# A two-layer hybrid decoder on one core: the 16x16 inverse in two halves of 8, and another order of the work beside it

## The chip, the core and the metric

The kernel runs on one core of a Trainium2 chip. Its time is device time in microseconds; the median of three runs is 1308.17 (1307.17 to 1308.69). The core has a matmul engine (PE; its weight loads are shown as PEld), a vector engine (DVE), a scalar engine (ACT), a general engine (POOL) and a queue that starts transfers (SP). Each works off its own list of instructions in order and waits on semaphores for the others.

## The reference, cut to what matters

256 tokens of width 1024 go through two layers, then a last norm. A layer is

```
x += 1/2 * SwiGLU(norm(x))
P  = norm(x) @ W_in                     # columns: RWKV-7 heads | MoBA q, k, v
x += concat[rwkv7(P_rwkv), moba(P_moba)] @ W_out
x += CrossAttn(norm(x), norm(mem))      # 4 heads over 256 memory tokens
x += 1/2 * SwiGLU(norm(x))
```

RWKV-7 has 8 heads of 64. For each head and token, with state S of 64x64:

```
S_t = S_{t-1} * decay_t + (S_{t-1} (-kk_t)) b_t^T + v_t k_t^T ;   y_t = S_t r_t
```

then a norm per head, a bonus term sum(r k r_k) v and a gate. MoBA has 8 heads of 64; with 256 tokens there is one block, so it is causal attention with a bias that depends on the distance of the tokens: softmax(q k^T / 8 + bias) v.

## The kernel before

**Matmuls.** Weights and activations are split into a high and a low part; a product is three matmuls (high x high, high x low, low x high). `load` fetches 1 MB of weights with one transfer on SP into one of two `raw` buffers, `unit` splits it in two halves of 1024 columns: ACT copies the high part (`whi`, line 83), DVE subtracts for the low part (`wlo`, line 77). `BANK(tag)` gives one of 8 PSUM banks: four `acc` for the dense products, two `tr` and two `pm`.

**RWKV in chunks.** The 256 tokens are four chunks of 64 (`rwkv`, line 568). `shifted` projects and mixes with the token before; `k, r, v, a, g` are tiles of 128 partitions (two heads of 64) by 4 pairs by 256 tokens. `kk` is normalized k; its squares `sq` are summed on PE into `pn`. `G` and `Gi` hold the decays and their inverses. `BK` (decayed keys) and `ZL` (decayed kk and r) are multiplied per chunk and head into 64x128 pair products, which masks (`C_MB`, `C_MK`) turn into `XB` and a part of `ZL` (lines 679 to 691).

A chunk needs the inverse of a triangular 64x64 matrix, 32 of them in all (4 chunks by 8 heads). `UD`/`UT` bring the 16x16 diagonal blocks into one layout, 128 partitions by 16 by 16 (`ub` the block, `mb` the inverse, from the identity), and all of them are inverted at once, one row after the other, lines 722 to 730:

```
for i in range(14, -1, -1):
    n = 15 - i                      # n == 1 is a copy
    tt(pr[:, 0:n, 0:n], mb[:, i + 1:16, i + 1:16], ub[:, i, None, i + 1:16] broadcast, mult)
    tensor_reduce(mb[:, i + 1:16, i:i + 1], pr, add)
    yield XI
```

`M` and `W2` are the inverses in matmul form; four steps of 32x32 matmuls (`p1`, `p2`/`p3`, `p4`, `p5`, line 762 on) combine them into 64x64 inverses `W`, first for chunks 0 and 1 (`cp = 0`), then for 2 and 3. Then `BV` (the bonus), and chunk by chunk: `from_state(0)` into `R`, `W` times `R`, `from_state(1)`, `BT` into the next state, `XB` for the output; after every second chunk the norm per head and the turn back into `yT`.

**The order of the work.** `rwkv` is a generator that yields, after each step, an amount of time that dense work may fill; `mix` (line 885) adds it up and takes pieces from a second generator until it is used up:

```
else:
    due += w
    while due > 0:
        due -= next(fill, 1e9)
```

Until the pair products are done the fill is `early`, MoBA's q and k projections. At `yield None` memory is split into an operand (`mem_operand`), and the fill becomes `others`: a piece of MoBA (`att`: `scores`, `turned`, `values` for each of four pairs of heads), after each a half unit of memory's keys (`late`, 24 matmuls of 256 columns), then memory's values `v_block(mT, 0)` (four pieces of 12 matmuls of 512 columns), then the first units of the output projection `og`. `v_block(mT, 1)` comes with the cross attention. A planner finally orders each engine's list by this order, and takes something later first where it reckons an engine would wait. `issue_after(i)` makes instructions queue behind `i` on its engine.

Of the kernel before, what the change touches and what calls it, by code (L numbers as in the profile page):

```python
# [16 lines left out]
S = 256  # L17
# [11 lines left out]
XI, XM, XC, XG = 0.3, 3.0, 1.2, 1.0  # L29
# [18 lines left out]
def body(tc, ctx, I, out):  # L48
# [27 lines left out]
    def tt(out_, a, b, op):  # L76
        V.tensor_tensor(out=out_, in0=a, in1=b, op=op)  # L77
# [7 lines left out]
    def split(hi, lo, src):  # L85
        c = copy(hi, src)
        tt(lo, src, hi.bitcast(FT), OP.subtract)
        return c.ins

# [305 lines left out]
    def mem_operand(m):  # L395
        mT = XT()
        for j in range(4):
            put_pair(mT, j, m[j // 2][:, 2 * (j % 2):2 * (j % 2) + 2, :])
        return mT
# [72 lines left out]
    def moba_bias():  # L472
        rel, oh = table
        u = SM([8, 384], name="u", tag="k2")
        V.memset(u[:, 256:384], NEG)
        p = BANK("pm")
        mm(p[0:8, 0:S], rel, oh)
        copy(u[:, 0:S], p[0:8, 0:S])
        nc.gpsimd.dma_start(scr_t, u)
        t = scr_t[:, :]  # L480
        nc.gpsimd.dma_start(scr_b, bass.AP(tensor=t.tensor, offset=t.offset, ap=[[0, 128], [1, 8 * 384]]))

    def moba(qT, kT, v, yT):
# [16 lines left out]
        def scores(p):  # L500
            load_bias(p + 1)
            s = [BANK("acc") for _ in range(2)]
            for t in range(2):
                for e in range(2):
                    r = half(e)
                    mm(s[e][:, cols[t]], qT[p // 2][r, p % 2, t * 128:(t + 1) * 128],
                       kT[p // 2][r, p % 2, 0:(t + 1) * 128])
            probs[p] = []
            for e in range(2):
                lg = SM([128, 384], name="lg", tag="k4")  # L510
                for t in range(2):
                    stt(lg[:, cols[t]], s[e][:, cols[t]], 0.125, bias[p][:, e, 128 * (1 - t):S],
                        OP.mult, OP.add)
                m = SM([128, 2], name="m", tag="n2")
                z = SM([128, 2], name="z", tag="n2")
                for t in range(2):
                    V.tensor_reduce(m[:, t:t + 1], lg[:, cols[t]], axis=AX.X, op=OP.max, negate=True)
                    A.activation(lg[:, cols[t]], lg[:, cols[t]], AF.Exp, bias=m[:, t:t + 1],  # L518
                                 accum_out=z[:, t:t + 1])
# [48 lines left out]
    def rwkv(l, xT, yT):  # L568
# [32 lines left out]
        for j in range(2):  # L601
            ac = BANK("acc").rearrange("p (c t) -> p c t", c=2)
            for c in range(2):
                p = 2 * j + c
                mm(ac[:, c, :], ups[:, 512 + p * 128:512 + (p + 1) * 128], wa[:, 1, :])
            for c in range(2):
                copy(G1[:, 2 * j + c, :], ac[:, c, :], scale=X(8, 2 * j + c))
            copy(g[:, 2 * j:2 * j + 2, :], ac)
        shifted(2, k[:, 2:4])

# [5 lines left out]
        V.memset(G[:, :, :, 0:1], 1.0)  # L616
# [44 lines left out]
        for cp in range(2):  # L661
            tt(BK[cp][:, :, :, 0:64], pv(a, cp), pv(Gi, cp), OP.mult)
            tt(BK[cp][:, :, :, 64:128], pv(km, cp), pv(Gi, cp), OP.mult)
        ZL = [[None, None] for _ in range(2)]
        for cp in range(2):
            Gp = G[:, :, 2 * cp:2 * cp + 2, :].rearrange("p c n t -> p n c t")
# [12 lines left out]
        for c in range(NCH):  # L679
            cp, cc = divmod(c, 2)  # L680
            pxs = [BANK(("pm", "tr")[cc]).rearrange("p (c t) -> p c t", c=4) for _ in range(2)]
            for p in range(4):
                for e in range(2):
                    hs = half(e)
                    mm(pxs[e][:, p, :], BK[cp][hs, cc, p, :], ZL[e][cp][hs, cc, p, :])
            for e in range(2):
                hs, ho = half(e), half(1 - e)
                px = pxs[e]
                tt(XB[cp][hs, cc], px[0:64], con[hs, None, C_MB:C_MB + 128].to_broadcast([64, 4, 128]),
                   OP.mult)  # L690
                tt(ZL[e][cp][ho, cc], px[64:128],
                   con[ho, None, C_MK:C_MK + 128].to_broadcast([64, 4, 128]), OP.mult)
# [14 lines left out]
        ub, mb, pr = (SM([128, 16, 16], name=n, tag="k1") for n in ("ub", "mb", "pr"))  # L707
# [4 lines left out]
        V.tensor_copy(mb, con[:, C_EYE:C_EYE + 256].rearrange("p (a b) -> p a b", a=16))  # L712
# [9 lines left out]
        for i in range(14, -1, -1):  # L722
            n = 15 - i
            if n == 1:
                V.tensor_copy(mb[:, 15, 14:15], ub[:, 14, 15:16])
                continue
            tt(pr[:, 0:n, 0:n], mb[:, i + 1:16, i + 1:16],
               ub[:, i, None, i + 1:16].to_broadcast([128, n, n]), OP.mult)
            V.tensor_reduce(mb[:, i + 1:16, i:i + 1], pr[:, 0:n, 0:n], axis=AX.X, op=OP.add)
            yield XI  # L730
        M, W2 = (SM([128, 16, 32], name=n, tag="k2") for n in ("M", "W2"))
        for z, zz in ((mb.rearrange("p a b -> p b a"), M), (mb, W2)):
# [3 lines left out]
            V.transpose(zz.rearrange("p n (b i) -> p i n b", b=2), ex.rearrange("p i b j -> p (i b j)"))  # L736
        W = H([128, 16, 64], name="W")
        for e in range(2):
            V.memset(W[e * 64 + 32:e * 64 + 64, :, 0:32], 0.0)
# [17 lines left out]
        values(0)  # L757
        for e in range(2):
            V.memset(SV[0][half(e), :, e, 0, :], 0.0)
        hq = [slice(e * 64, e * 64 + 32) for e in range(2)]  # L760
        hr = [slice(e * 64 + 32, e * 64 + 64) for e in range(2)]
        for cp in range(2):
# [3 lines left out]
            p1 = BANK("pm")[:, 0:256].rearrange("p (c t) -> p c t", c=8)  # L766
# [5 lines left out]
            p3 = BANK("tr")[:, 0:256].rearrange("p (c t) -> p c t", c=8)  # L772
            p2 = BANK("pm")[:, 0:256].rearrange("p (c t) -> p c t", c=8)
# [20 lines left out]
            p5 = BANK("pm")[:, 0:256].rearrange("p (c t) -> p c t", c=8)  # L794
# [6 lines left out]

        for j in range(2):
# [7 lines left out]
        for c in range(NCH):  # L810
# [14 lines left out]
            values(c + 1)  # L825
# [27 lines left out]
            if cc == 0:  # L853
                y = SM([128, 2, 4, 64], name="y", tag="k2")
            copy(y[half(1), cc], pz[half(1), :, 0, :])
            copy(y[half(0), cc], pz[half(0), :, 1, :])
            if cc == 0:
                continue
# [25 lines left out]

    def mix(l, xT, post):
# [277 lines left out]
```

## Time and profile before

| | |
|---|---|
| median of three runs | 1308.17 us |
| profiled execution, its own time | 1309.38 us |
| its span, first to last instruction | 1307.4 us |
| PE busy | 1282.3 us (98%), 8710 matmuls |
| PEld busy | 1099.3 us (84%) |
| DVE busy | 919.9 us (70%), 1709 instructions |
| ACT busy | 761.1 us (58%), 1447 instructions |
| POOL busy | 58.0 us (4%) |
| mean granted clock of PE | 0.993 |

A busy matmul engine isn't one at its peak: matmuls overlap, and their ends are modelled. Where a helper records an operation, all its uses have one line (77 is `tt`, 80 `stt`, 83 `copy`, 94 `mm`), so a row is told by its tiles. The mixing stage with RWKV and MoBA lies at 204 to 408 us in the first layer and at 850 to 1050 in the second. In all that follows, times are us from the start of the span.

### The profile page before, as it was taken

How to read it: one execution, taken by the hardware profiler on the slowest of the kernel's cores; microseconds unless marked ns; L12 is line 12 of the kernel's file. 1: busy time of each engine (PE TensorE's matmuls, PEld its weight loads, DVE VectorE, ACT ScalarE, POOL GpSimd, SP SyncE). 2: the span in 40 equal slices, each digit the busy share in tenths (PEclk: the TensorE clock that was granted, in tenths of full speed). 3: DMA queues.
4: the chain of work that ended last, by engine and by line, in shares of the span. 5: the costliest groups of instructions: out<-in, count | busy, mean ns of one | idle time of the engine just before them, and what ended most of it. 6: DMA issues, size and time to landing. Idle time of an engine off the chain costs nothing.

```text
span 1307.4 us, 21984 instructions
## 1 busy us (share of the span) xinstructions
PE 1282.3 (98%) x8710; PEld 1099.3 (84%) x8710; DVE 919.9 (70%) x1709; ACT 761.1 (58%) x1447; POOL 58.0 (4%) x61
## 2 busy tenths in 40 slices
PE   8999999998999999999999999999999999999997
PEld 6888888997778888888888888899887798888886
DVE  6797557797688767765576665668976877766644
ACT  6656437658646565564465554474785555655543
POOL 0081000020000000000000000000200000000000
PEclk9999999998999999999999999999999999999999
DMA  7867663333235345555635556443442345355552
GB/s 276 322 233 252 210 225 130 130 129 123 107 129 179 129 144 195 191 194 188 230 129 193 192 178 222 165 135 124 138 155 82 130 161 177 131 192 194 181 176 94
DMA packets 34422, 224.36 MB, mean 172 GB/s; under 512 B 4328, under 2 KB 4752, under 8 KB 9104
## 3 DMA queue, kind: packets, MB, share of 16 engines
q1 hardware_dynamic: 31344, 212.93, 46.4%
q0 software_dynamic: 2400, 9.45, 2.1%
q8 instruction: 68, 1.11, 0.3%
q10 hardware_dynamic: 576, 0.59, 0.1%
q14 instruction: 34, 0.28, 0.1%
HBM read 219.80 MB, written 4.73 MB: 172 GB/s over the span
## 4 chain that ended last, share of the span: by engine, by line
PE 77%; DVE 11%; ACT 7%; DMA 2%; issue 2%; SPq 0%; ACTq 0%
PE acc L94 71%; PE pm L94 4%; DVE wlo L77 3%; DMA raw<-in_w_f1i_dram 2%; DVE ZL L77 2%; ACT whi L83 1%; PE tr L199 1%; DVE XB L77 1%; DMA raw<-in_w_k_dram 1%; ACT BT L83 1%; ACT lg L518 1%; DVE wb L77 0%; ACT W L83 0%; DVE rkv L80 0%; DVE z L77 0%
## 5 line engine op out<-in xcount | busy, mean ns | idle before, releaser
L94 PE MATMUL acc<-xt,whi 128*128 128x512 f32 (+1 forms) x2496 | 685.0, 345 | 3.1 <-DVE lg L80 2.4
L77 DVE TENSOR_TENSOR wlo<-raw,whi 128x1024 fp32r<-128x1024 f32 (+1 forms) x456 | 465.3, 1036 | 260.5 <-ACT whi L83 259.0
L83 ACT ACTIVATE whi<-raw 128x1024 fp32r<-128x1024 f32 (+1 forms) x456 | 403.7, 905 | 325.5 <-PE acc L94 234.7
L94 PE MATMUL acc<-xt,wlo 128*128 128x256 f32 x1888 | 532.2, 283 | 2.2 <-DVE wlo L77 2.2
L94 PEld LDWEIGHTS acc<-xt,whi 128*128 128x128 f32 x2496 | 435.2, 191 | 67.6 <-DVE lg L80 2.9
L94 PEld LDWEIGHTS acc<-xt,wlo 128*128 128x128 f32 x1888 | 360.2, 191 | 4.5 <-DVE wlo L77 3.7
L94 PE MATMUL acc<-whi,hT 128*128 128x512 f32 x704 | 220.6, 393 | 0.0
L94 PEld LDWEIGHTS acc<-whi,hT 128*128 128x128 f32 x704 | 132.3, 188 | 30.0
L94 PE MATMUL acc<-wlo,hT 128*128 128x512 f32 x352 | 138.3, 393 | 0.0
L94 PEld LDWEIGHTS acc<-wlo,hT 128*128 128x128 f32 x352 | 66.2, 188 | 14.7
L77 DVE TENSOR_TENSOR z<-acc,z 128x256 f32<-128x256 f32 x160 | 66.8, 417 | 2.2 <-ACT z L83 2.2
L94 PE MATMUL acc<-wb,xt 128*128 128x512 f32 x240 | 62.0, 400 | 0.0
L83 ACT ACTIVATE z<-acc 128x256 f32<-128x256 f32 x160 | 58.5, 366 | 2.9 <-PE acc L94 2.9
L94 PE MATMUL acc<-whi,xt 128*128 128x512 f32 x160 | 53.4, 408 | 2.5 <-ACT whi L83 2.0
L83 ACT ACTIVATE xt<-tr,par 128x128 fp32r<-128x128 f32 x112 | 38.5, 365 | 27.9 <-PE tr L199 16.2
L94 PEld LDWEIGHTS acc<-wb,xt 128*128 128x128 f32 x240 | 43.3, 188 | 9.6 <-ACT xt L83 0.7
L174 ACT ACTIVATE junk<-x 128x512 f32<-128x512 f32 x36 | 22.7, 631 | 46.6 <-DVE x L80 25.2
L83 ACT ACTIVATE hT<-z 128x256 fp32r<-128x256 f32 x80 | 32.4, 405 | 18.6 <-DVE z L77 18.6
L77 DVE TENSOR_TENSOR z<-z,z 128x256 f32<-128x256 f32 x80 | 36.5, 456 | 7.3
L80 DVE SCALAR_TENSOR_TENSOR xt<-tr,par,xt 128x128 fp32r<-128x128 f32 x112 | 36.1, 345 | 7.8 <-ACT xt L83 7.8
L94 PE MATMUL acc<-whi,oT 128*128 128x512 f32 x128 | 40.3, 393 | 0.0
L94 PEld LDWEIGHTS acc<-whi,xt 128*128 128x128 f32 x160 | 29.9, 190 | 11.3 <-ACT whi L83 3.4
(249 smaller groups left out, 1224.0 us busy)
## 6 DMA issues: line engine op xcount, KB each, us to landing
raw<-in_w_f2i_dram SPq DMA_DIRECT2D x44, 1024.0 KB, 4.8
raw<-in_w_f1i_dram SPq DMA_DIRECT2D x42, 1024.0 KB, 4.9
raw<-in_w_f1o_dram SPq DMA_DIRECT2D x22, 1024.0 KB, 4.8
raw<-in_w_mixa_dram SPq DMA_DIRECT2D x22, 1024.0 KB, 4.8
raw<-in_w_f2o_dram SPq DMA_DIRECT2D x22, 1024.0 KB, 4.8
raw<-in_w_k_dram SPq DMA_DIRECT2D x8, 1024.0 KB, 4.8
raw<-in_w_v_dram SPq DMA_DIRECT2D x8, 1024.0 KB, 4.9
raw<-in_w_mixo_dram SPq DMA_DIRECT2D x8, 1024.0 KB, 4.9
```

The costliest lines, as they stand in the source:

```text
L77: V.tensor_tensor(out=out_, in0=a, in1=b, op=op)
L80: V.scalar_tensor_tensor(out_, a, s, b, op0=op0, op1=op1)
L83: return A.activation(out_, in_, AF.Copy, **k)
L94: nc.tensor.matmul(o, a, b, start=start, stop=stop, skip_group_check=True)
L174: marks["square"] = A.activation(junk, xt[:, n * 512:(n + 1) * 512], AF.Square, scale=1.0 / 32.0, accum_out=ss[:, n:n + 1]).ins
L199: nc.tensor.transpose(p[:, k, :], xs[:, k * 128:(k + 1) * 128], ident)
L518: A.activation(lg[:, cols[t]], lg[:, cols[t]], AF.Exp, bias=m[:, t:t + 1], accum_out=z[:, t:t + 1])
```

## The change

- The inverse treats each 16x16 block as two 8x8 blocks on the diagonal, inverted both at a time (views `ud`, `md`, sizes 2 x n x n, n up to 7), and the 8x8 block below as a product of three, two passes of 512 elements each with a reduction. `ub` and `mb` lie in one tile.
- `others` now starts with `v_block(mT, 0)` and two units of keys; then MoBA, with a half unit of keys after every third piece. `XI` and `XM` change; the inverse yields `2 * XI` a step. The first product of the inverse queues behind `mem_operand`'s last subtraction.
- The second half of the 32x32 stage becomes a generator of its own, `second`, advanced one step after each yield of chunks 0 and 1. Its banks are `tr` instead of `pm`.
- The pair products: each 64x128 matmul becomes two of 64x64, so that all masked products of `XB` land in one bank and need one masking pass.
- `kk` and `sq` come ahead of the scan; `ZL` by full products and copies; `BV` in `km`'s buffer and behind the inverse; some memsets and copies go to POOL, `G1` to DVE.
- MoBA: the bias table is stored times 8, and one `tensor_tensor_reduce` adds it and finds the maximum; the division goes from ACT to DVE. `v_block(mT, 1)` sums in `pm`.

The diff, cut to its core:

```
-XI, XM, XC, XG = 0.3, 3.0, 1.2, 1.0
+XI, XM, XC, XG = 0.8, 2.6, 1.2, 1.0
...
+            marks["memory"] = tt(mT[j][:, :, 1, :], src, mT[j][:, :, 0, :].bitcast(FT), OP.subtract).ins
...
-                for t in range(2):
-                    stt(lg[:, cols[t]], s[e][:, cols[t]], 0.125, bias[p][:, e, 128 * (1 - t):S],
-                        OP.mult, OP.add)
...
-                    V.tensor_reduce(m[:, t:t + 1], lg[:, cols[t]], axis=AX.X, op=OP.max, negate=True)
+                    V.tensor_tensor_reduce(lg[:, cols[t]], s[e][:, cols[t]], bias[p][:, e, 128 * (1 - t):S],
+                                           -0.125, -NEG, OP.add, OP.min, m[:, t:t + 1])
...
-                    copy(lg[:, cols[t]], lg[:, cols[t]], scale=z[:, t:t + 1])
+                    V.tensor_scalar(lg[:, cols[t]], lg[:, cols[t]], z[:, t:t + 1], None, op0=OP.mult)
...
+            tt(two(kk), two(kk), Gp(0), OP.mult)
+            tt(two(rG), two(r), Gp(1), OP.mult)
...
-                tt(ZL[e][cp][hs, :, :, uc(e)], pv(kk, cp)[hs], Gp[hs, :, :, 0:64], OP.mult)
-                tt(ZL[e][cp][hs, :, :, dc(e)], pv(r, cp)[hs], Gp[hs, :, :, 1:65], OP.mult)
+                copy(ZL[e][cp][hs, :, :, uc(e)], pv(kk, cp)[hs])
+                copy(ZL[e][cp][hs, :, :, dc(e)], pv(rG, cp)[hs])
...
-                    mm(pxs[e][:, p, :], BK[cp][hs, cc, p, :], ZL[e][cp][hs, cc, p, :])
+                    for i in range(2):
+                        mm(pxs[i][half(e ^ i), p, :], BK[cp][hs, cc, p, half(i)], ZL[e][cp][hs, cc, p, :])
+            tt(XB[cp][:, cc], pxs[0], con[:, None, C_MB:C_MB + 128].to_broadcast([128, 4, 128]), OP.mult)
...
-        for i in range(14, -1, -1):
-            n = 15 - i
+        for i in range(6, -1, -1):
+            n = 7 - i
...
+            pr = SM([128, 2, n, n], name="pr", tag="k1")
+            with after([marks["memory"]] if n == 2 else []):
+                tt(pr, md[:, :, i + 1:8, i + 1:8],
+                   ud[:, :, i, None, i + 1:8].to_broadcast([128, 2, n, n]), OP.mult)
+            V.tensor_reduce(md[:, :, i + 1:8, i], pr, axis=AX.X, op=OP.add)
+            yield 2 * XI
...
+        tt(pr, mb[:, hi, None, hi].to_broadcast([128, 8, 8, 8]),
+           ub[:, None, lo, hi].to_broadcast([128, 8, 8, 8]), OP.mult)
+        V.tensor_reduce(um2, pr, axis=AX.X, op=OP.add)
+        yield 2 * XI
...
+        V.tensor_reduce(mb[:, hi, lo], pr, axis=AX.X, op=OP.add)
...
-        for cp in range(2):
+        def inverse(cp):
...
-            p1 = BANK("pm")[:, 0:256].rearrange("p (c t) -> p c t", c=8)
+            p1 = BANK("tr")[:, 0:256].rearrange("p (c t) -> p c t", c=8)
...
+        yield from inverse(0)
+        second = inverse(1)
+
+        BV = km
+        for p in range(4):
+            with after([marks["inverse"]]):
+                stt(BV[:, p, :], r[:, p, :], P(P_RK, p), km[:, p, :], OP.mult, OP.mult)
...
+        for c in range(NCH):
+            for w in chunk(c):
+                yield w
+                if c < 2:
+                    next(second, None)
...
-            acc = [BANK("acc") for _ in range(2)]
+            acc = [BANK(("acc", "pm")[n]) for _ in range(2)]
...
         def others(mT):
+            yield from v_block(mT, 0)
             ks = late(mT)
-            for w in att:
+            yield from islice(ks, 4)
+            for i, w in enumerate(att):
                 yield w
-                yield from islice(ks, 1)
+                if i % 3 == 1:
+                    yield from islice(ks, 1)
             yield from ks
-            yield from v_block(mT, 0)
```

## Rows read from the trace of the kernel before

**Rows 1.** The page's chain of work that ended last, by engine.
```profile
PE 77%; DVE 11%; ACT 7%; DMA 2%; issue 2%; SPq 0%; ACTq 0%
```
**Rows 2.** Whom PE waited for, whole span: total us, times, longest us.
```profile
PE acc L94 <- ACT mpT L83: 2.7, 2, 1.4
...
PE acc L94 <- DVE lg L80: 2.4, 2, 1.2
...
PE pm L94 <- ACT sq L625: 1.6, 2, 1.0
...
PE acc L530 <- DVE lg L80: 0.6, 2, 0.4
```
**Rows 3.** Stretches: length, busy PE, PEld, DVE, ACT, POOL (instructions), clock, DMA, GB/s.
```profile
240.00:250.00 10.00, 10.00 (x74) 10.00 (x74) 7.37 (x20) 6.38 (x12) 0.00 (x0) 0.83 0.39 141
255.00:290.00 35.00, 34.22 (x302) 32.88 (x301) 33.51 (x56) 17.69 (x25) 7.90 (x8) 1.00 0.36 122
...
300.00:310.00 10.00, 6.85 (x90) 5.85 (x89) 9.68 (x30) 9.91 (x25) 0.73 (x1) 1.00 0.40 132
310.00:320.00 10.00, 9.75 (x245) 8.15 (x232) 8.02 (x17) 7.62 (x20) 0.71 (x1) 0.84 0.62 216
320.00:330.00 10.00, 10.00 (x221) 9.37 (x220) 4.60 (x6) 6.80 (x14) 0.00 (x0) 0.82 0.19 63
...
340.00:377.00 37.00, 36.88 (x419) 27.34 (x415) 26.89 (x57) 21.20 (x42) 0.55 (x1) 1.00 0.22 73
...
901.00:936.00 35.00, 34.22 (x302) 32.87 (x301) 33.87 (x57) 17.81 (x25) 7.76 (x8) 1.00 0.38 127
...
946.00:956.00 10.00, 7.21 (x118) 6.38 (x119) 9.67 (x27) 9.91 (x24) 0.73 (x1) 1.00 0.40 131
```
**Rows 4.** Timeline of DVE: the first and the last step of the inverse.
```profile
288.57 0.16 DVE L77 TENSOR_TENSOR pr<-mb,ub 128x4 f32<-128x4 f32 x1
...
306.80 0.39 DVE L77 TENSOR_TENSOR pr<-mb,ub 128x225 f32<-128x225 f32 x1
```
**Rows 5.** Timeline around `sq`, ACT's and PE's: start, us, instruction, idle before.
```profile
232.00 1.04 ACT L619 ACTIVATE Gi<-Lc 128x1024 f32<-128x1024 f32 x1
...
237.43 1.06 ACT L625 ACTIVATE sq<-kk 128x1024 f32<-128x1024 f32 x1 [0.55 <-DVE kk L623]
...
238.54 1.95 PE L94 MATMUL pm<-con,sq 128*128 128x2 f32 x16 [0.96 <-ACT sq L625]
```
**Rows 6.** DVE's groups, 204 to 420: count, busy us, mean ns, idle before.
```profile
L77 DVE TENSOR_TENSOR ZL<-kk,G 64x512 f32<-64x512 f32 x4 | 2.7, 684 | 0.1
L77 DVE TENSOR_TENSOR XB<-pm,con 64x512 f32<-64x512 f32 x4 | 2.7, 684 | 0.1
```
**Rows 7.** Groups of DVE and ACT, 204 to 420: logits and the value copies.
```profile
L80 DVE SCALAR_TENSOR_TENSOR lg<-acc,bp 128x256 f32<-128x256 f32 x8 | 3.3, 414 | 0.0
L517 DVE TENSOR_REDUCE m<-lg 128x1 f32<-128x256 f32 x8 | 3.3, 407 | 0.0
...
L83 ACT ACTIVATE SV<-tr 64x512 f32<-64x512 f32 x8 | 4.7, 590 | 0.1
...
L83 ACT ACTIVATE lg<-lg,z 128x256 f32<-128x256 f32 x8 | 4.0, 497 | 0.0
```
**Rows 8.** Timeline of POOL: products of 256 columns.
```profile
75.47 8.59 POOL L386 TENSOR_SCALAR memG<-memT,par 128x256 f32<-128x256 f32 x5
```
**Rows 9.** Timeline of PE: pair products, and the steps of a chunk (two rows a matmul).
```profile
267.36 1.16 PE L94 MATMUL tr<-ZL,BK 64*128 64x128 f32 x16
268.45 0.50 PE L94 MATMUL acc<-xt,whi 128*128 128x256 f32 x2
...
360.81 0.68 PE L94 MATMUL pm<-R,W 64*64 64x64 f32 x16
361.42 0.69 PE L94 MATMUL pm<-SV,ZL 128*64 128x64 f32 x16
362.04 0.50 PE L94 MATMUL acc<-whi,xt 128*128 128x512 f32 x1
```

More of the change, by code (lines that the diff above doesn't have):

```diff
@@ L76, in tt @@
     def tt(out_, a, b, op):
-        V.tensor_tensor(out=out_, in0=a, in1=b, op=op)
+        return V.tensor_tensor(out=out_, in0=a, in1=b, op=op)
     def stt(out_, a, s, b, op0, op1):
@@ L88, in split, with in_two @@
         return c.ins
+    def in_two(z):
+        return z[:, 0:256], z[:, 256:512]
     def after(ins):
@@ L397, in mem_operand @@
         for j in range(4):
-            put_pair(mT, j, m[j // 2][:, 2 * (j % 2):2 * (j % 2) + 2, :])
+            src = m[j // 2][:, 2 * (j % 2):2 * (j % 2) + 2, :]
+            copy(mT[j][:, :, 0, :], src)
+            marks["memory"] = tt(mT[j][:, :, 1, :], src, mT[j][:, :, 0, :].bitcast(FT), OP.subtract).ins
         return mT
@@ L477, in moba_bias @@
         mm(p[0:8, 0:S], rel, oh)
-        copy(u[:, 0:S], p[0:8, 0:S])
+        copy(u[:, 0:S], p[0:8, 0:S], scale=8.0)
         nc.gpsimd.dma_start(scr_t, u)
@@ L606, in rwkv @@
             for c in range(2):
-                copy(G1[:, 2 * j + c, :], ac[:, c, :], scale=X(8, 2 * j + c))
+                V.tensor_scalar(G1[:, 2 * j + c, :], ac[:, c, :], X(8, 2 * j + c), None, op0=OP.mult)
             copy(g[:, 2 * j:2 * j + 2, :], ac)
         shifted(2, k[:, 2:4])
+        kk = H([128, 4, S], name="kk")
+        sq = H([128, 4, S], name="sq")
+        for p in range(4):
+            V.tensor_scalar(kk[:, p, :], k[:, p, :], X(0, p), None, op0=OP.mult)
+        A.activation(sq, kk, AF.Square, scale=1.0 / RS)
         Lc = H([128, 4, S], name="Lc")
@@ L663, in rwkv @@
             tt(BK[cp][:, :, :, 64:128], pv(km, cp), pv(Gi, cp), OP.mult)
+        rG = H([128, 4, S], name="rG")
         ZL = [[None, None] for _ in range(2)]
         for cp in range(2):
[L666 removed]
+            Gp = lambda i: G[:, :, 2 * cp:2 * cp + 2, i:i + 64]
+            two = lambda z: ch(z)[:, :, 2 * cp:2 * cp + 2, :]
+            tt(two(kk), two(kk), Gp(0), OP.mult)
+            tt(two(rG), two(r), Gp(1), OP.mult)
             for e in range(2):
@@ L706, in rwkv @@
         V.transpose(UT.rearrange("p i b j -> p (i b j)"), UD.rearrange("p i n c b -> p (i n c b)"))
-        ub, mb, pr = (SM([128, 16, 16], name=n, tag="k1") for n in ("ub", "mb", "pr"))
+        both = SM([128, 512], name="both", tag="k2")
+        ub, mb = (z.rearrange("p (a b) -> p a b", a=16) for z in in_two(both))
+        ud, md = (z.rearrange("p (x r) -> p x r", x=2)[:, :, c:c + 128].rearrange(
+            "p x (a b) -> p x a b", a=8)[:, :, :, c:c + 8] for z, c in ((both[:, 0:272], 0), (both[:, 240:512], 8)))
         par2 = [con[:, C_PAR + i:C_PAR + i + 1] for i in range(2)]
@@ L735, in rwkv @@
                 V.tensor_scalar(ex[:, :, b, :], z, par2[b], None, op0=OP.mult)
-            V.transpose(zz.rearrange("p n (b i) -> p i n b", b=2), ex.rearrange("p i b j -> p (i b j)"))
+            marks["inverse"] = V.transpose(zz.rearrange("p n (b i) -> p i n b", b=2), ex.rearrange("p i b j -> p (i b j)")).ins
         W = H([128, 16, 64], name="W")
         for e in range(2):
-            V.memset(W[e * 64 + 32:e * 64 + 64, :, 0:32], 0.0)
+            nc.gpsimd.memset(W[e * 64 + 32:e * 64 + 64, :, 0:32], 0.0)
         SV = []
@@ L757, in rwkv @@
         values(0)
+        values(1)
         for e in range(2):
-            V.memset(SV[0][half(e), :, e, 0, :], 0.0)
+            nc.gpsimd.memset(SV[0][half(e), :, e, 0, :], 0.0)
         hq = [slice(e * 64, e * 64 + 32) for e in range(2)]
         hr = [slice(e * 64 + 32, e * 64 + 64) for e in range(2)]
-        for cp in range(2):
+        def inverse(cp):
             ix = slice(cp * 8, cp * 8 + 8)
@@ L771, in rwkv @@
             yield XM
-            p3 = BANK("tr")[:, 0:256].rearrange("p (c t) -> p c t", c=8)
-            p2 = BANK("pm")[:, 0:256].rearrange("p (c t) -> p c t", c=8)
+            p2, p3 = (z.rearrange("p (c t) -> p c t", c=8) for z in in_two(BANK("tr")))
             for i in range(8):
@@ L800, in rwkv @@
             yield XM
+        yield from inverse(0)
+        second = inverse(1)
+        BV = km
+        for p in range(4):
+            with after([marks["inverse"]]):
+                stt(BV[:, p, :], r[:, p, :], P(P_RK, p), km[:, p, :], OP.mult, OP.mult)
         for j in range(2):
@@ L808, in rwkv, with chunk @@
             stt(BV[:, p, :], BV[:, p, :], P(P_LNB, p), g[:, p, :], OP.add, OP.mult)
-        for c in range(NCH):
+        ys = []
+        def chunk(c):
             cp, cc = divmod(c, 2)
@@ L824, in rwkv @@
             V.tensor_copy(R[half(1)], pz[half(1), :, 1, :])
-            values(c + 1)
+            if c:
+                values(c + 1)
             yield XC
@@ L857, in rwkv @@
             if cc == 0:
-                continue
+                return
             y = y.rearrange("p n c t -> p (n c) t")
```

38 lines of the change are left out of this document (15 added, 23 removed).

## The prediction

> **What bounds the kernel now.** I read the page's chain of waits first, then PE's own waits, then busy time by stretch, and went into single instructions only where these pointed. The chain lies 77% on PE [rows 1], so a microsecond saved elsewhere counts only where PE waits for it. PE's waits for MoBA are three entries, two occurrences each, one per layer: 2.7 us for `mpT` (turned probabilities), 2.4 and 0.6 us for `lg` (logits) [rows 2]. Together 5.7 us. Next, 1.6 us for `sq`. The stretches show why [rows 3]. From 255 to 290 (pair products beside dense fill) PE is busy 34.22 of 35 us although DVE is at 33.51: DVE is full, but PE has other work. From 300 to 310 (inverse on DVE, MoBA as fill) PE falls to 6.85 of 10 with DVE at 9.68 and ACT at 9.91: the fill itself needs the two engines that the inverse occupies. Layer 1 repeats it, 7.21 of 10 from 946. In 340 to 377 (recurrences beside dense products) PE is at 36.88 of 37. So what can be won are some 5.7 us of MoBA's waits, a few small ones, and stretches at half clock: the granted clock is 0.83 in 240 to 250, and 0.84 and 0.82 in 310 to 320 and 320 to 330, each next to narrow matmuls or waits.
>
> The profile's own execution took 1309.38 us (span 1307.4), 1.2 above the median 1308.17. The sum is made against 1309.4 and brought down by 1.2 at the end.
>
> **The inverse.** Now 14 steps of a product and a reduction, from 0.16 us each at 4 elements to 0.39 us at 225 [rows 4]: about 1.04 ns an element above a floor of 0.16. Summed over the sizes, 28 instructions take some 6.9 us. After: six steps with 8, 18, 32, 50, 72, 98 elements, 12 instructions of 0.16 to 0.26, some 2.4 us; and four of 512 elements, by the same slope 0.16 + 0.53 = 0.69, some 2.8 us. 5.2 against 6.9: 1.7 us of DVE and 12 instructions fewer, bounds 0 to 2.7. That alone moves the end by nothing, since PE is what ends late; the gain is from what runs beside it.
>
> **The fill.** Under the inverse PE gets four pieces of the value product and four of keys ahead of MoBA, instead of logits. These need only weight splits, as the fill of 255 to 290 does, where PE ran at 34.22 of 35. So all 5.7 us of waiting leave this place. They don't all leave the kernel: the same logits, exponentials, turns and products now stand between the steps of the state recurrences, with only four key pieces as dense work between them, and each step there ends on a DVE or ACT copy too. Bounds: all 5.7 stays away, or all returns. I take half, -2.9, as there is a key piece between every scores and its turn, but none between a turn and its values. By the Trainium skill (page "Trainium Kernel Development and Optimization", section "Performance Expectations") a matmul's busy time tells little and the busy share of weight loads is what to judge by. By that share, 32.88 of 35 as full rate and 5.85 and 6.38 of 10 in the two bad stretches, the loss is 6.6 us rather than 5.7 and half of it 3.3; the trace agrees in place and nearly in size.
>
> **Waits that are added.** The first product of the inverse must queue on DVE behind memory's four low halves (512 columns, so about 0.69 each, 2.8 us), and these wait for buffers that the last dense matmuls of the stretch before free. Behind it on DVE stands the rest of the inverse; PE waits for that only at its products, after six to eight dense pieces. So 0; if DVE's list outlasts the pieces, up to 2.8 us a layer. `BV` must queue behind the inverse's last transpose, and `W` gets its buffer only when `BV` has read r: W is first wanted two product steps later, 0. The weight loads on SP keep their number and size, values before keys; POOL's bias loads move with MoBA and nothing on POOL that is wanted in this stage queues behind them: 0.
>
> **Earlier key norms.** `kk` and `sq` are asked for ahead of the scan and exponentials. Now PE waits 0.96 us for a `sq` that ACT starts at 237.43; the copies of k's second half, from which it is made, queue on ACT behind the exponentials, the last at 232.00 [rows 5]. Without those in front the chain ends one exponential (1.04 us) or more earlier, which covers the wait. I take the whole 1.6 us of both layers [rows 2]: -1.6, bounds 0 and -1.6.
>
> **DVE ahead of the inverse.** The masks are applied once over 128 partitions instead of twice over 64: 4 x 0.68 us less a layer. Decayed `ZL` is made by 4 full products for 8 half ones (0.68 each [rows 6]), also 2.7 us less, and 8 copies on ACT of about 0.59 each [rows 7], 4.7 us, more. Four `BV` products move behind the inverse, memsets go to POOL, four `G1` scalings come from ACT to DVE (some 1.4 us). DVE's 33.51 of 35 [rows 3] falls to about 27, ACT's 17.69 rises to about 22: neither is then full. PE's idle 0.78 us in this stretch, twice (255 to 290 and 901 to 936), goes: -1.6, bounds 0 and -1.6. POOL's new work hides in its idle time; if not, the identity comes late by one pass, some 1.7 us for 256 columns (8.59 for five [rows 8]).
>
> **MoBA's softmax.** 16 additions and 16 maxima (0.41 us each for 256 columns, less for 128 [rows 7]) become 16 fused passes. The trace has no such pass: at least one, 0.41, at most both, 0.82. I take 0.5, as an addition is the nearer row. 16 scalings go from ACT (0.50) to DVE. DVE thus keeps its load and ACT is eased by some 7 us. PE: nothing beyond what the fill's term holds.
>
> **Pair products.** 8 matmuls of 64 rows by 128 columns a chunk become 16 of 64 by 64, for the same columns streamed: the array must hold four tiles at once to break even. A chunk now takes 1.09 us to the next matmul (267.36 to 268.45 [rows 9]). `R,W`, eight 64x64 matmuls on two tiles with 64 columns, takes 0.61 (360.81 to 361.42); twice the matmuls at twice the columns is at worst 4 x 0.61 = 2.44. So 0 to +1.35 a chunk, eight chunks: 0 to +10.8 us; nothing below zero, since four tiles at best stream as long as two did. `SV,ZL` takes 0.62 with two column tiles over the same rows, so tiles do run side by side in both directions; nearer the low end: +0.25 x 8 = +2.0.
>
> **Clock.** The half-speed stretch of 310 to 330 costs (0.16 + 0.18) x 10 = 3.4 us in the profiled execution, and follows the worst waits. With dense fill it may go: half, -1.7, bounds 0 and -3.4. That of 240 to 250 sits behind matmuls of two columns that stay: 0, bound -0.17 x 10 = -1.7 a layer if layer 1 has it too.
>
> **The tail.** MoBA's last pair now ends after the recurrences and the output projection waits for it. Cover: the last key piece and the second value product, which now uses other banks. 0; uncovered, turn, copy and product of one pair, about 2 us a layer.
>
> **Sum:** -2.9 - 1.6 - 1.6 + 2.0 - 1.7 = -5.8; 1309.4 - 5.8 = 1303.6, less 1.2: **1302 us**.
>
> **Rivals.**
> 1. *The waits move to the recurrences and grow.* Behind the first inverse lie 11 recurrence steps and 4 of the second inverse, each ended by a copy on an engine that now also runs all of MoBA. For it: 300 to 310 shows what MoBA beside a DVE chain does to PE. Against it: the chain there was 28 instructions long on one engine, and a recurrence step has one or two. At 0.5 us a step, 15 steps, two layers: +15, and none of the fill's or the clock's gain: 1309.4 + 15 - 3.2 + 2.0 - 1.2 = 1322. It decides from 0.2 us a step: 6 us, the whole gain.
> 2. *The pair products run two tiles at a time.* +10.8 in place of +2.0: 1311, slower. For it: `R,W` has two row tiles only, and no row shows four 64x64 tiles. Against it: `R,W` and `SV,ZL` together. The Trainium skill ("TensorEngine Tiling (Array Packing)", section "Gotcha 1: PSUM Pressure") says that different row tiles cannot access the same PSUM bank at once, and after the change they do, where before each had its bank. By that rule the price is this rival's. The trace speaks against it: `R,W` writes one bank from both row tiles, and is as fast as `SV,ZL`, which has no second row tile.
> 3. *All waits and the half-speed stretches go:* -5.7 - 3.2 - 3.4 - 3.4, products at no cost: 1309.4 - 15.7 - 1.2 = 1292.5.
> 4. *No net:* fill's waits return in full, the clock stays: -3.2 + 2.0: 1307.
>
> **Chances.** About 0.2% (2.6 us) can be told from no change. Forecast (1296 to 1305.5) 0.50; rival 3, 0.14; rival 4, 0.15; rival 2, 0.09; rival 1, 0.12, of which smaller sizes end at 1310 to 1316. Faster is the forecast and rival 3: 0.64; same rival 4 and the edge of 2: 0.17; slower the rest: 0.19. The range, 1291 to 1312, leaves out the far part of rival 1 and the extremes.
>
> **What would show it.** Right: no wait for `lg` or `mpT` under the inverse, PE above 9.4 of 10 there; no wait for `sq`; pair products near 1.1 to 1.4 us a chunk. Wrong: pair products at 2 us or more; DVE above 9 of 10 and PE below 9 in the recurrences; new half-clock stretches there; PE idle at the output projection.

## The result, and the profile after

The changed kernel took 1316.2 us (median; 1310.4 to 1318.2) beside 1308.69 for the kernel before on the same chip: ratio 1.0056, 95% interval 1.0029 to 1.0083. In a later session (e14 below) it was 1.0042, 1.0020 to 1.0063. So it is about half a per cent slower, where the forecast said faster. The profiled execution took 1312.45 us (span 1310.1, before 1307.4). Its mean granted clock is 0.993, and the four of the seven executions that took over 1316 us have 0.986 to 0.992, so the trace shows 2.7 us of a loss that is 7.5 in the median.

The chain by engine hardly moved [rows 1], but TensorE's waits did. The rows after, as in [rows 2] (total us, times, longest us):
```profile
PE tr L97 <- ACT T L83: 7.7, 4, 4.5
...
PE tr L97 <- DVE M L756: 3.1, 2, 1.6
PE tr L97 <- issue: 2.7, 1, 2.7
PE pm L97 <- ACT R L83: 2.4, 2, 1.4
PE acc L97 <- DVE xt L77: 1.6, 1, 1.6
...
PE pm L97 <- DVE z L523: 0.6, 2, 0.3
```
The waits for `mpT`, `lg` and `sq` are gone, 7.3 us; in their place stand `T` (the inverse's first copied product), `M` (what VectorE's inverse delivers; 1.0 before) and others, 18.1 us.

Next the stretches, first before and then after, from the first transposes of `BK` (the inverse's start) to the first product with `yr` (the output projection), layer 0 and layer 1; columns as in [rows 3]:
```profile
289.80:382.40 92.60, 88.92 (x1187) 73.03 (x1186) 68.74 (x161) 66.43 (x153) 3.99 (x6) 0.96 0.36 126
935.30:1025.40 90.10, 86.14 (x1187) 70.44 (x1186) 68.50 (x160) 66.15 (x153) 1.45 (x2) 1.00 0.33 112
```
```profile
285.20:381.60 96.40, 89.12 (x1194) 76.01 (x1193) 71.80 (x185) 59.32 (x135) 5.63 (x10) 0.96 0.35 121
928.60:1030.40 101.80, 89.64 (x1194) 76.12 (x1194) 73.57 (x186) 61.55 (x138) 3.10 (x6) 0.97 0.29 100
```
This one stage went from 182.7 to 198.2 us, 15.5 longer: TensorE's idle time in it rose from 7.6 to 19.4 us, its busy time from 175.1 to 178.8. What lies around it gave 12.8 back, nearly all in three places: the inverse starts 4.7 us earlier in layer 0 and is reached 3.5 us faster from there to layer 1, and the output projection behind is 2.3 and 2.0 us shorter, as less fill is left for it (198 and 197 products against 204 and 205). 15.5 - 12.8 is the 2.7 us between the spans. The loss is therefore in the stage of inverse and recurrences. 11.7 of the 15.5 us are layer 1's. There TensorE waits 4.45 us for `T`, and it stands 2.71 us where the profile shows nothing that it waits for:
```profile
956.37 0.84 PE L97 MATMUL tr<-T,W 32*32 32x32 f32 x29 [4.45 <-ACT T L83]
...
983.22 0.18 PE L97 MATMUL tr<-M,XB 32*32 32x32 f32 x1 [2.71 <-issue]
```

How the waits come about is read from three engines of layer 0. VectorE: the inverse starts (292.18) only behind memory's last split `xt`, and that behind a weight split that stood 2.19 us; `BV`'s four products by r (written into `km`) end at 306.77.
```profile
290.44 1.23 DVE L77 TENSOR_TENSOR wlo<-raw,whi 128x1024 fp32r<-128x1024 f32 x1 [2.19 <-ACT whi L83]
291.58 0.69 DVE L77 TENSOR_TENSOR xt<-memT,xt 128x512 fp32r<-128x512 f32 x1
292.18 0.16 DVE L77 TENSOR_TENSOR pr<-both 128x8 f32<-128x8 f32 x1
...
301.79 1.04 DVE L756 STREAM_TRANSPOSE M<-ex 128x512 f32<-128x512 f32 x1
...
305.19 1.58 DVE L80 SCALAR_TENSOR_TENSOR km<-rkv,par,km 128x256 f32<-128x256 f32 x4
```
ScalarE: weights that came late, and then the first split of memory's values, which starts 0.03 us after the last of `BV`'s four has ended. Nothing in that split needs `BV`'s result: `v` is being written into the buffer that r had. `T` is queued behind it.
```profile
289.35 1.06 ACT L83 ACTIVATE whi<-raw 128x1024 fp32r<-128x1024 f32 x1 [3.57 <-DMA raw<-in_w_k_dram]
...
306.80 0.60 ACT L83 ACTIVATE v<-acc 128x512 fp32r<-128x512 f32 x1 [2.56 <-DVE km L80]
307.30 1.05 ACT L83 ACTIVATE whi<-raw 128x1024 fp32r<-128x1024 f32 x1
308.37 2.40 ACT L83 ACTIVATE SV<-tr 64x512 f32<-64x512 f32 x4
310.79 0.38 ACT L83 ACTIVATE T<-tr 128x256 f32<-128x256 f32 x1
```
TensorE waits for `M`, then for `T`, and comes to chunk 0's product `R,W` at 339.32, where W is the last to arrive; that first product of the recurrences stood at 341.1 before.
```profile
302.97 0.74 PE L97 MATMUL tr<-M,UA 32*32 32x32 f32 x64 [1.65 <-DVE M L756]
...
311.23 0.83 PE L97 MATMUL tr<-T,W 32*32 32x32 f32 x29 [2.95 <-ACT T L83]
...
320.53 0.69 PE L97 MATMUL tr<-W,TB 32*32 32x32 f32 x32
...
339.32 0.29 PE L97 MATMUL pm<-R,W 64*64 64x64 f32 x2 [0.41 <-ACT W L83]
```
W is late because GpSimd clears its tile at 337.12 (layer 1: 985.94), although the products that fill it were done at 321:
```profile
337.12 1.09 POOL L759 MEMSET W<- 32x512 f32 x2 [5.99 <-issue]
```

**Theory H (slots).** Tag `e`, the scratch pool, has 14 buffers of 4 KB. Counted in the code, 14 tiles are alive at the inverse after the change: v, g, G1, G, km, r, four `ZL`, two `XB`, two `BT`. r and km are among them because `BV` moved behind the inverse. Three more are asked for: the two tiles of memory's values, which the new fill asks for first, and W. The slots come free as r (read by `BV`, 306.8), g (about 327) and v (about 336), and are given in the order of asking: first value tile, second value tile, W. **Theory F**, the rival, is the prediction's first: the recurrences have too little dense fill, whatever the slots.

### The profile page after: what moved, and what is told of

Its sections match the earlier page's. It is cut to its first block, busy times and chain, and to the rows that moved or that the text cites. A ratio compares the mean times of both kernels' runs of the same rounds, so it can differ in the third digit from the quotient of the medians.

```text
span 1310.1 us, 22248 instructions
## 1 busy us (share of the span) xinstructions
PE 1276.6 (97%) x8838; PEld 1101.1 (84%) x8838; DVE 910.0 (69%) x1697; ACT 756.7 (58%) x1423; POOL 51.3 (4%) x73
## 4 chain that ended last, share of the span: by engine, by line
PE 77%; DVE 10%; ACT 6%; DMA 3%; issue 3%; SPq 0%; ACTq 0%; DVEq 0%
PE acc L97 69%; PE pm L97 5%; DVE wlo L77 3%; ACT whi L83 2%; DMA raw<-in_w_f1i_dram 2%; PE tr L202 1%; PE tr L97 1%; DMA raw<-in_w_k_dram 1%; DMA raw<-in_w_mixa_dram 1%; ACT ZL L83 1%; ACT BT L83 1%; ACT UD L83 1%; ACT SV L83 0%; DMA raw<-in_w_o_dram 0%; ACT lg L521 0%
## 5 line engine op out<-in xcount | busy, mean ns | idle before, releaser
L83 ACT ACTIVATE xt<-tr,par 128x128 fp32r<-128x128 f32 x112 | 38.5, 366 | 28.5 <-PE tr L202 15.5
L77 DVE TENSOR_TENSOR hT<-z,hT 128x256 fp32r<-128x256 f32 x80 | 35.5, 443 | 3.2 <-ACT hT L83 3.2
L358 ACT ACTIVATE z<-z 128x256 f32<-128x256 f32 x80 | 32.7, 409 | 4.3 <-DVE z L77 4.3
```

Of the source, the lines that this page charges most:

```text
L77: return V.tensor_tensor(out=out_, in0=a, in1=b, op=op)
L83: return A.activation(out_, in_, AF.Copy, **k)
L358: A.activation(sums[0], sums[0], AF.Silu)
```

## The experiments

Medians in us, ratio to the kernel before on the same chip with its 95% interval; from the profiled run TensorE's waits for `T` in both layers, when W is cleared in layer 0, and the length of the stage above, both layers.

| kernel | median | ratio | T | W | stage |
|---|---|---|---|---|---|
| changed | 1316.2 | 1.0056 (1.0029 to 1.0083) | 7.7 | 337.1 | 198.2 |
| e14 changed again | 1311.6 | 1.0042 (1.0020 to 1.0063) | 9.2 | 336.7 | 196.2 |
| e9 no order | 1306.4 | 1.0010 (0.9991 to 1.0029) | 0.3 | 333.6 | 193.5 |
| e5 less room, 14 slots | 1305.9 | 0.9998 (0.9975 to 1.0021) | 4.7 | 334.7 | 189.4 |
| e10 BV early, 14 slots | 1303.4 | 0.9987 (0.9971 to 1.0003) | 0.3 | 334.3 | 188.4 |
| e13 15 slots | 1296.3 | 0.9927 (0.9905 to 0.9948) | 3.6 | 325.0 | 179.3 |
| e2 keys first, 14 slots | 1295.8 | 0.9936 (0.9914 to 0.9958) | none | 308.1 | 186.4 |
| e1 16 slots | 1293.7 | 0.9907 (0.9879 to 0.9935) | 1.3 | 307.3 | 178.0 |
| e11 keys first, 16 slots | 1289.4 | 0.9874 (0.9851 to 0.9897) | 0.4 | 288.8 | 171.6 |

The trace of e2 is of an execution of 1302.3 us, 6.5 above its median, so its stage is not to be set against that median.

**e1, sixteen slots.** Against the changed kernel:
```diff
-WB = 5
-HEAP = {"e": 14, ...
-SMALL = {"k1": 6, ...
+WB = 4
+HEAP = {"e": 16, ...
+SMALL = {"k1": 5, ...
```


> The changed kernel, whole, but the scratch pool of 4 KB buffers (tag e) has 16 slots in place of 14; the room comes from one weight buffer (5 to 4) and one small buffer (k1, 6 to 5). Theory H (slots): 14 tiles of that pool are alive at the inverse, because r and km now live until BV, which stands behind the inverse's last transpose; memory's two value tiles and W find no slot, the first split of the values holds ScalarE 2.56 us ahead of T, and W's clearing waits until v(rkv) is read at 336.7. With 16 slots TensorE's wait for T (3.1 and 4.6 us) falls under 1 us in both layers, GpSimd clears W before 312 (layer 0) instead of at 337.1, chunk 0's product with W starts 8 to 15 us earlier than 339.3, and the time is 1300 to 1308. Theory F (the fill is too thin in the recurrences, whatever the slots): the waits change places and the time stays at 1316, plus or minus 3; fewer weight buffers could add to it under either.


1293.67 us. W is cleared as soon as `BV` has read r, and `R,W` follows at 324.9 (GpSimd, then TensorE's wait, e1):
```profile
307.32 1.09 POOL L759 MEMSET W<- 32x512 f32 x2 [18.62 <-DVE km L80]
...
324.91 0.77 PE L97 MATMUL pm<-R,W 64*64 64x64 f32 x16
```
H holds; F falls, since the same pieces of fill are used and 1.5% of the time is gone (1.0056 to 0.9907). How much of that is the slots' is seen with e5. The time is even below H's range.

**e5, room only**, the control: WB 4 and k1 5 with 14 slots.


> Control for e1: the changed kernel with one weight buffer and one small buffer fewer (WB 4, k1 5), as e1 has them, but the scratch pool left at 14 slots. Theory H: the waits of the changed kernel stay (T 3 to 5 us in each layer, W cleared at about 337 in layer 0), 1316 plus or minus 5. Theory N (what helped e1 was the other buffering of weights, not the slots): 1294 to 1303.


1305.86: a miss for both. Slots at equal room are thus worth 12.2 us (e5 to e1), not the whole, and with them goes another order of TensorE's list, which the planner makes (some 1000 of its 8838 records stand elsewhere in e1's trace than in e5's). The rest came by another way: VectorE's and ScalarE's instructions stand in another order there, the key weights are not waited for ahead of the inverse (at 303.26 they are, for 2.85 us), the inverse starts 2.7 us earlier and `BV` begins at 302.45, so the same chain is shorter. No run parts these. VectorE in e5:
```profile
287.75 1.22 DVE L77 TENSOR_TENSOR wlo<-raw,whi 128x1024 fp32r<-128x1024 f32 x1
288.88 0.69 DVE L77 TENSOR_TENSOR xt<-memT,xt 128x512 fp32r<-128x512 f32 x1
289.49 0.16 DVE L77 TENSOR_TENSOR pr<-both 128x8 f32<-128x8 f32 x1
```
The wait for `M`, that for `xt` and the 2.71 us of layer 1 are gone and `T` is at 4.7; W is as late as it was.

**e2, keys first**: 14 slots, nothing changed but the order of the fill.
```diff
-            yield from v_block(mT, 0)
-            ks = late(mT)
-            yield from islice(ks, 4)
+            yield from late(mT)
+            vs = v_block(mT, 0)
...
-                    yield from islice(ks, 1)
-            yield from ks
+                    yield from islice(vs, 1)
+            yield from vs
```


> The changed kernel with another order of the fill only: all eight key pieces of memory first, then MoBA with the pieces of the first half of memory's values between its steps, the rest of them behind. The two value tiles are so asked for later, W's clearing goes ahead of them, and no value split stands ahead of T on ScalarE. Theory H: the wait for T falls under 1 us, W is cleared as soon as r is read (about 307), chunk 0's product with W starts 8 us or more ahead of 339.3, and the time is 1302 to 1310. Theory F: even less dense fill is left for the recurrences than in the changed kernel (MoBA there instead), so 1316 to 1322.


1295.83. With 14 slots and all weight buffers, W now stands ahead of the value tiles and gets r's slot at 308.1; no split stands before `T`. F said 1316 or more.

**e10, BV early**: only the four products by r move, to behind the `ZL` loop.


> The changed kernel (14 slots) with BV's four products by r moved from behind the inverse's last transpose to ahead of the pair products, so r's slot comes free long before the inverse. Theory H: the first split of memory's values has its slot at once, ScalarE no longer stands 2.56 us ahead of T, the wait for T falls under 1.5 us a layer; the second split and W still wait for the slots of g and v(rkv) (about 325 and 334), so W stays late: 1303 to 1311. If the wait for r is not what holds T, T's waits stay at 3 us and more and the time at 1316, plus or minus 3.


1303.35, as H has it: `T`'s waits are 0.3 us, W is still late. It is 0.55 to 0.7% under the changed kernel (7 to 9 us, from 1.0042 or 1.0056 to 0.9987). That is at most the price of r's slot, since the waits for `M` and `xt` (3.1 and 1.6 us) are gone as well. How late W may cost without a large wait of its own: TensorE fills the time to 336 with other products, and then chunk 1 stands close behind chunk 0 with only a few of MoBA's products between. TensorE in e10:
```profile
309.24 0.38 PE L97 MATMUL tr<-W,T 32*32 32x32 f32 x21 [1.49 <-issue]
...
341.15 0.69 PE L97 MATMUL pm<-SV,ZL 128*64 128x64 f32 x16 [0.19 <-DVE SV L77]
343.20 1.28 PE L97 MATMUL pm<-R,W 64*64 64x64 f32 x16 [1.36 <-ACT R L83]
344.41 1.12 PE L97 MATMUL pm<-SV,ZL 128*64 128x64 f32 x16
...
975.65 1.01 PE L97 MATMUL acc<-mqk,mqk 64*128 64x256 f32 x2 [2.79 <-issue]
```
The stage is 10.4 us longer than in e1, but that is not the price of late W: TensorE stands 1.49 and 2.79 us (first and last line) where the profile shows nothing that it waits for, and the granted clock behind is 0.67 in 310 to 315, 0.55 in 975 to 980 and 0.77 in 980 to 985, by these figures some 5 us more. W's slot is better priced by e13 and e5, which have no such stand over 0.4 us. At 344.41 sixteen products take 1.12 us that take 0.69 at 341.15. That the spell of half clock follows the waits is what the rows show; that late W is what brings it is argued, not shown by itself.

**e13, fifteen slots**, between e5 and e1.


> The changed kernel with WB 4 and k1 5, as e5 and e1, and 15 slots, between them. By the order in which slots come free, the first value tile takes the 15th slot at once, so no split stands on ScalarE ahead of T (T's waits under 1.5 us in all, as e1); the second takes r's, and W takes g's, read last by BV's closing products at about 325: W cleared at 323 to 331, against 307 in e1 and 335 in e5. Time between the two: 1296 to 1303. If the slots' order is not the cause, it is as e5 (1304 to 1308) or as e1 (1292 to 1295) with W's clearing where it is there.


1296.28. W takes g's slot, just as the order of asking says, when `BV`'s closing products have read it (ScalarE's second value split, on r's slot, then GpSimd; e13):
```profile
305.89 0.60 ACT L83 ACTIVATE v<-acc 128x512 fp32r<-128x512 f32 x1 [0.30 <-DVE km L80]
...
325.00 1.09 POOL L759 MEMSET W<- 32x512 f32 x2 [2.91 <-DVE km L80]
```
`T`'s waits, 3.6 us, missed the forecast: the second split stands ahead of `T`. The 15th slot brings 9.6 of the 12.2 us, with W ten us earlier and `T`'s waits 1.1 us shorter. The stage in e5, then in e13, columns as in [rows 3]:
```profile
286.50:380.30 93.80, 88.89 (x1194) 76.09 (x1192) 69.67 (x180) 58.94 (x133) 5.62 (x10) 0.96 0.35 121
930.20:1025.80 95.60, 90.36 (x1194) 77.33 (x1192) 69.66 (x180) 59.08 (x133) 3.14 (x6) 0.95 0.30 103
```
```profile
286.50:376.90 90.40, 86.00 (x1195) 74.13 (x1194) 71.41 (x184) 59.55 (x134) 5.67 (x10) 0.98 0.34 117
926.30:1015.20 88.90, 84.56 (x1194) 72.71 (x1194) 71.39 (x184) 59.57 (x134) 3.10 (x6) 1.00 0.29 101
```
10.1 us between them: TensorE's busy time 8.7, for the same products at a higher granted clock (0.98 and 1.00 against 0.96 and 0.95), and idle time 1.4. The rest of W's earliness buys little, since `R,W` is at 327.1 here and 324.9 in e1.

**e9, no order**: the inverse no longer held behind memory's splits; VectorE's order differs, a few of ScalarE's instructions, and nothing else.
```diff
-            with after([marks["memory"]] if n == 2 else []):
+            with after([]):
```


> The changed kernel without the order that holds the inverse's last small step behind memory's splits; only VectorE's list changes, every other engine's work stands in the same order. In the changed kernel VectorE stood 2.19 us at a weight split (its weights reached ScalarE 3.57 us late), memory's last split came behind it, and the inverse began at 292.18; TensorE then waited 1.65 and 1.5 us for M. Without the order the inverse begins at about 287 and M comes 1 to 2 us earlier, but memory's splits come about 4 us later. If the order is part of the loss: M's waits go and nothing takes their place, 1309 to 1313. Theory H holds it for small: TensorE waits for memory's split xt in place of M, T's waits stay above 2 us, 1313 to 1320.


1306.38, better than either said. As forecast, `xt` takes `M`'s place; but the inverse now starts at 282.7, `BV` is done by 301.4, r's slot is free early enough that `T`'s wait goes (e9):
```profile
PE acc L97 <- DVE xt L77: 7.2, 2, 3.6
PE tr L97 <- issue: 2.5, 1, 2.5
...
PE tr L97 <- ACT T L83: 0.3, 2, 0.2
```
So the order and the slot are one chain: late weights, memory's last split, inverse, `BV`, r's slot, value split, `T`.

**e4 and e8, the old fill** (a key piece after each MoBA step, values last, prices 0.3 and 3.0) on 14 and on 16 slots.


> The changed kernel with the fill in the order of before (a key piece after each MoBA step, memory's values last) and the two planner prices of before (0.3 and 3.0); the new inverse, the late BV, the fused softmax and the early front stay. Theory H: the value tiles are asked for last, so the wait for T falls under 1 us; r and km still live long, so W may still wait for a slot; 1300 to 1306. Theory F: the dense fill is back in the recurrences, 1299 to 1303. Against the front alone (e3) the difference is then what inverse, softmax and late BV are worth without the new fill: under H 0 to +4 us, under F 0 to -3.

> e1 with the fill of before (a key piece after each MoBA step, memory's values last, planner prices 0.3 and 3.0): what the new order of the fill is worth once slots are there. e4, the same on 14 slots, took 1302.9. If the new fill is what wins (MoBA's own waits under the inverse gone, as the prediction's term says), 1297 to 1302, 3 us or more over e1. If it is worth nothing and slots alone decide, 1292 to 1296.


1302.91 (0.9986, 0.9966 to 1.0006) and 1301.92 (0.9971, 0.9948 to 0.9994): where the values are asked for last, two more slots and the room taken for them make no difference that can be told. As H has it, `T` is not waited for in either, and W is cleared at 310.04 in e4 already (287.67 in e8). And with slots enough the new fill with its prices is worth 8.2 us (e8 to e1).

**e7, the old inverse** in e1.


> e1 with the inverse of before (one 16-row substitution in 14 steps in place of two of 8 and a product); the rest as e1. The prediction put the inverse at 0 by itself. VectorE's part was 6.9 against 5.2 us, and it stands in front of M, for which TensorE has fill: under the prediction's term 1292 to 1296, no difference to e1 that can be told. If the inverse's end is what sets the recurrence's start there, +2 to +6 (1296 to 1300), and the first product with M comes 2 us or more later than e1's 303.3.


1296.53 (0.9925, 0.9903 to 0.9947): 2.9 us over e1, with intervals that overlap. The first product with `M` comes 1.5 us later than in e1 (304.75 against 303.28), where 2 or more would have shown that the inverse's end sets the time. The wait that the shorter inverse saves is in the trace of e7, where e1 has none over 0.2 us:
```profile
PE tr L97 <- DVE M L745: 4.3, 2, 2.2
```

**e3, the front only**: the kernel before with the parts ahead of the inverse.


> The kernel before with only the part of the change that lies ahead of the inverse: G1 on VectorE, key norms earlier, the products with G over whole blocks and the 64x64 pair products. Inverse, fill, MoBA's softmax and BV as before. Both theories: what lies ahead of the inverse gained 4.7 us in layer 0 and 3.9 in layer 1 between the two profiled runs, so 1300 plus or minus 2. If it stays at 1306 or more, the early gain is not one that lasts and both theories are short of a piece.


1306.32 (0.9996, 0.9978 to 1.0014): a miss. The inverse started at 286.77, 3.1 us earlier, but the next attention's first scores came at 419.7 against 419.3. The stage from the inverse to those scores holds 1390 products in both and takes 132.9 us against 129.5: TensorE idles 2.3 us more, `xt` among its waits, and is busy 1.1 us longer at a granted clock of 0.96 against 0.97. The new copies into `ZL` were waited for, too, and MoBA's waits of [rows 2] stayed (the trace is of an execution of 1310.8 us):
```profile
PE pm L94 <- ACT ZL L83: 3.4, 4, 1.1
PE acc L94 <- ACT mpT L83: 3.0, 2, 1.5
...
PE acc L94 <- DVE lg L80: 2.5, 4, 1.1
```

**e12, the old pair products** and products with G in e1.


> e1 with the pair products of before (128 rows at a time, 16 records a chunk) and the products with G of before, on VectorE by halves; no rG, no ScalarE copies into ZL. The prediction priced the new form at +2.0 us (bounds 0 to +10.8): if that were right, this one is 2 us under e1, 1292. The traces say otherwise: 32 records of 64 rows went by in 0.83 us where 16 of 128 took 1.09, 2.1 us less over eight chunks, with 1.6 us of waits for ScalarE's copies on the other side: then e12 is 0 to 4 us over e1, 1294 to 1298.


1302.21 (0.9969, 0.9953 to 0.9985), 8.5 over e1. The expectation's 0.83 us was measured to the start of the last record; to the next product, as the prediction did, it is 1.03. So the products are not what e12 loses. VectorE does the products with G by halves again, and `wlo` is waited for 6.8 us against 1.6 in e1, 5.2 of the 8.5.
```profile
PE acc L97 <- DVE wlo L77: 6.8, 5, 2.3
```

**e6, before with 16 slots**, WB 4, k1 5.


> Control for e1: the kernel before with the sizes of e1 (16 slots, WB 4, k1 5). Theory H: r was read before the inverse there, no tile waited for a slot around the inverse, so 1306 plus or minus 4. Theory N: the larger pool helps any version of the kernel, and it comes out 6 us or more below the kernel before.


1324.13 (1.0137, 1.0091 to 1.0182). Theory N falls: the larger pool does not help by itself. H's 1306 missed as well: these sizes cost the kernel before 18 us, where one weight buffer fewer did the changed kernel good (e5). The order of the work differs, `yr` is waited for 6.4 us, the mean clock is 0.987 against 0.993; why is open. So the sizes alone can move the time by more than the slots are priced at, through the order of the work. That slots are what held `T` and W rests on the releasers in the traces and on e1, e2, e10, e11 and e13, which all gain on the changed kernel; the single prices are less sure.

**e11, keys first and sixteen slots.**


> The candidate for the best: 16 slots as in e1 and the fill of e2 (key pieces first). Under H both take away the same waits, so there is nothing left for the second to win: 1291 to 1297, as e1. If the order of the fill has a gain of its own (e2 had its slots in time only by that order), 1286 to 1291.


1289.41, 1.3% under the kernel before and the best. A free slot is there at once (W cleared at 288.84), and TensorE is busy for 84.90 of 85.70 us at full clock:
```profile
287.30:373.00 85.70, 84.90 (x1195) 71.91 (x1194) 68.24 (x181) 58.06 (x133) 5.68 (x10) 1.00 0.39 132
921.70:1007.60 85.90, 85.06 (x1195) 72.09 (x1195) 68.35 (x181) 58.10 (x133) 3.10 (x6) 1.00 0.33 115
```
It is 4.3 us under e1, with intervals that overlap, so keys first may have a gain of its own, and e2's gain need not be the slots' alone.

**e14, the changed kernel again.**


> The changed kernel itself once more, on the same chip and in the same rounds as e13: 1316 plus or minus 4, 0.4 to 0.8 % over the kernel before; T's waits 6 to 9 us in all and W cleared at 335 to 339. If it comes out under 1309, part of the difference between the two kernels was the chip's and not theirs.


1311.61; the loss repeats, though 4.6 us smaller in the median, and a little under the 1312 that was the least expected.

## Why the prediction was wrong, point by point

**The step that failed** is *Waits that are added*: "`BV` must queue behind the inverse's last transpose, and `W` gets its buffer only when `BV` has read r: W is first wanted two product steps later, 0." It saw the wait and followed it to the wrong tile. r's slot went to memory's values, whose split stands ahead of `T`, and W waited for v's, until 337. The step asked when W is wanted, not who else asks for a slot before it. The runs price this at 12.2 us for two slots at equal room (e5 to e1), 9.6 of it for the first (e13); r's slot by itself is at most 7 to 9 (e10). The step put 0. Its first half, the inverse behind memory's splits, had nearly the right bound (2.8 us a layer): the wait for `M` is 1.6 and 1.5, and 1.6 for `xt` comes on top in layer 1. What was missed there is that the key weights came late (3.57 us on ScalarE), and by e5 and e9 that delay is part of the same chain.

*The fill*, -2.9: right in sign and too small, 8.2 us by e8 and e1 (prices included), but only where slots are there. In the changed kernel itself TensorE is busy 14.35 of 16 us under the inverse (287 to 303), below the 9.4 of 10 that would have shown the forecast right. The Trainium skill's weight-load share ("Trainium Kernel Development and Optimization", "Performance Expectations"), 3.3 us for this term, erred the same way.

*The inverse*, 5.2 us of VectorE and 0 by itself: its four passes of 512 (two products, two reductions) took 0.69, 0.69, 1.07 and 0.69, near the 0.69 of the forecast. By e7 it may be worth some 3 us rather than 0, since its end is waited for; the intervals overlap.

*Earlier key norms*, -1.6: right, the product with `sq` follows without a wait at 237.00. *DVE ahead of the inverse*: VectorE at 29.51 of 35 us, TensorE at 35.00 (27 and full were forecast; [rows 3]), in TensorE's wait -1.6 as said. By e12 the relief is worth more, some 8 us in that plan, and by e3 nothing where the stage behind has its old waits.
```profile
250.00:285.00 35.00, 35.00 (x379) 33.48 (x378) 29.51 (x41) 24.09 (x35) 2.69 (x9) 1.00 0.42 151
287.00:303.00 16.00, 14.35 (x82) 12.22 (x80) 12.77 (x28) 9.37 (x18) 0.61 (x2) 1.00 0.43 165
303.00:320.00 17.00, 14.05 (x261) 13.52 (x262) 10.26 (x15) 8.59 (x13) 0.00 (x0) 0.80 0.36 125
```
*MoBA's softmax*: the fused pass takes 0.42 us at 256 columns, the price of one of the two it replaces [rows 7] (0.5 was taken).
```profile
L519 DVE CUSTOM_DVE_ANT_0 lg<-acc,bp 128x256 f32<-128x256 f32 x8 | 3.4, 420 | 0.0
```
*Pair products*, +2.0: too dear. A chunk takes 1.03 us against 1.09 [rows 9], so 0, a little under the bound that "nothing below zero" set; rival 2 falls.
```profile
264.34 1.10 PE L97 MATMUL tr<-ZL,BK 64*64 64x128 f32 x32
265.37 0.50 PE L97 MATMUL acc<-xt,whi 128*128 128x256 f32 x2
```
*Clock*, -1.7: wrong. The granted clock is 0.80 in 303 to 320, behind the waits for `M` and `T`; the rows above show it. In e11, with both waits gone, it is 1.00 in both layers.

Rival 1 had the right end (slower) by another mechanism: what PE waits for in the recurrences (`R`, 2.4 us) is small. Rival 3, everything hidden, at 1292.5 lies near e1's 1293.7, but that kernel has other sizes and its gain is made up otherwise, so the nearness is chance.

## What to carry to other kernels

When a change lengthens a tile's life, count the tiles alive in its pool at that moment and write down who asks next, in order: the wait lands on the first to ask and on everything queued behind it on its engine, not on the tile one has in mind. In a trace this shows as an instruction released by one whose result it doesn't read. And a gain ahead of a stage that is limited by its own waits is spent there: what counts is TensorE's idle time and its time at half clock over the whole span, not an earlier start. Changing a buffer count also changes a planned order, so a control at equal room is needed before a price is named.

## What the runs showed of the hardware

64x64 products on four tiles of the array, two row tiles writing one bank (different halves of its partitions), run side by side: 32 with 128 columns took 1.03 us, no longer than 16 on 64x128 of the array, a bank for each row tile (1.09). The Trainium skill's rule cited for rival 2 ("TensorEngine Tiling (Array Packing)", "Gotcha 1: PSUM Pressure") says that different row tiles cannot access one bank at the same time. No price of that is seen here; the measurement decides.

A product of 512 elements on VectorE took 0.69 us with operands read in order or broadcast (295.06 in the changed kernel), and 1.07 where one was read transposed (298.14, `pr<-um,both`).

TensorE sometimes stood with nothing in the profile that it waited for ("issue" in the rows above): once, 2.5 to 3.0 us in layer 1 in the products after `T`, in the changed kernel, e14 and e9; 1.5 and 2.8 us in e10, 1.9 in e2, 1.2 and 1.5 in e6. In e1, e5, e11 and e13 no such stand is over 0.4 us, so part of what these gain over the changed kernel may be this. What it is stays open.
